# Sums of weight quadrants made in DRAM by transfers that add, in place of additions on VectorE

## The chip, the cores and the metric

The kernel runs on one core of one Trainium2 chip, as one program with one launch. The metric is the time of one execution on the device in microseconds, the median over runs; lower is better.

## The reference

One layer of a hybrid trunk on x of 1024 tokens by 1024 channels, float32 throughout. What bears on this case is the input projection and what reads it:

```python
u = rms_norm(h, norm_w)
proj = u @ w_in
q, f_logit, i_in, g_hg, u_pool, g_pool, xbc, dt_raw, z = jnp.split(
    proj, [int(v) for v in np.cumsum(IN_SPLITS)[:-1]], axis=-1)
o_hg = group_rms_norm(hgrn2_mixer(q, f_logit, i_in, lb), hg_norm_w, HG_HEADS) * jax.nn.silu(g_hg.astype(jnp.float32))
o_pool = pool_mixer(u_pool, pool_w, pool_scale) * jax.nn.silu(g_pool.astype(jnp.float32))
y_ssd = ssd_mixer(xbc, dt_raw, conv_w, conv_b, dt_bias, a_log, d_skip) * jax.nn.silu(z.astype(jnp.float32))
...
h = h + mixed @ w_out
gate = jax.nn.sigmoid(h @ w_pg)
return h + gate * (p_i @ w_pe)
```

w_in has 6668 columns. The change concerns the 1024 columns of u_pool and g_pool (four pairs of 128-column blocks) and 1024 of the columns of z and g_hg (two pairs of 256-column blocks).

## The kernel before, in words

Every float32 operand of a product is split into a high part, rounded to the matmul type (a CAST on ScalarE, L139), and a remainder (a subtraction on VectorE, L140). `mm3` (L163) then makes three matmuls per block: high by high, and each high by the other remainder. uh and ul hold the two parts of the normalised, transposed u, 8 row tiles of 128 tokens.

**The start.** x is loaded in 8 row tiles by SP. For a tile t, `x_norm` (L196) takes the sum of squares on ScalarE (L198), makes the factor rsx on POOL in two small steps, a tensor_scalar and a power (`rstd`, L124, lines L126 and L127), and multiplies on VectorE (L200). `x_turn` (L202) transposes the tile on PE (L208) and splits it into uh and ul (L216, L217). `tm_tile` then makes the tile's first product, the first slab of values. The order of VectorE, ScalarE and POOL in this part is written by hand for its own instructions (`manual_schedule`, L242): the sum of squares of tile t+3 stands behind the splitting of tile t+1. PE's order is transposes of tile t+1, then the product of tile t. Everything after the first slab needs all 8 tiles.

**The Strassen stage.** Six products of u with pairs of column blocks are made with 7 half-size products each in place of 8. u is taken in quadrants; `build_sums` (L281) makes four sums of u's quadrants and splits them. For the weights, with the quadrants b11, b12, b21, b22, four sums are needed: t1 = b12 - b11, t3 = b22 - b12, t2 = t3 + b11, t4 = b21 - t2. `st_cm_w(j0, j1)` (L307) loads two blocks and makes the sums on VectorE (L315, L316, L319, L320) between the splits, for the pairs (26, 27), (30, 31), (28, 29), (32, 33). `st_cm` (L327) makes the seven products and puts them together from PSUM with copies on ScalarE (L340) and additions on VectorE (L344). `st_tm(s0, s1, fin)` (L361) does the same for the two pairs of 256-column blocks, (5, 6) and (7, 2), with its own loads into the arena `big` (L368) and additions at L373.

**Queues.** Raw weights come through `wload` (L130), two buffers of 128x1072, and the split parts go to four buffers each of hi and lo. The arena hands out the slab that has been free longest; whoever writes it waits for its last reader. Stores to pod (L529) and vd (L229) and loads share the queue of SP. Outside of the start a scheduler sets each engine's order; `high_priority` (L138, L314, L318, L343, L372) pulls splits, additions and evacuations forward in it. POOL issues no transfer in this kernel; besides the powers it only fills a few tiles.

Of the kernel before, what the change touches and what calls it, by code (L numbers as in the profile page):

```python
# [77 lines left out]
def body(ctx: ExitStack, tc: tile.TileContext, x, pT, wcm, wtm, wdt, wo, wg, we, nw, fw, cst, prm, out):  # L78
# [228 lines left out]
    def st_cm_w(j0, j1):  # L307

        r0, r1 = wload(wcm[j0], 1024), wload(wcm[j1], 1024)
        b11, b21, b12, b22 = r0[:, :512], r0[:, 512:1024], r1[:, :512], r1[:, 512:1024]  # L310
        T_, Th = bg.take(2048)
        t1, t3, t2, t4 = (T_[:, i * 512 : i * 512 + 512] for i in range(4))
        w0 = wsplit(r0, 1024)
        with tc.high_priority(offset=WPRIO):  # L314
# [2 lines left out]
        w1 = wsplit(T_[:, :1024], 1024)
        with tc.high_priority(offset=WPRIO):  # L318
            V.tensor_tensor(out=t2, in0=t3, in1=b11, op=ALU.add)  # L319
            V.tensor_tensor(out=t4, in0=b21, in1=t2, op=ALU.subtract)  # L320
        w2 = wsplit(T_[:, 1024:], 1024)
        w3 = wsplit(b22, 512)
        bg.give(Th)
# [3 lines left out]
    def st_cm(W, o0, o1):  # L327
# [27 lines left out]
        add_(o1[:, h1], X)  # L355
# [1 line left out]
        add_(o1[:, h0], Y)
# [3 lines left out]
    def st_tm(s0, s1, fin):  # L361

        src = lambda s, i: wtm[s * 2 + i]
        taken = []

        def load(s, i):
            z, h = bg.take(1024)
            nc.sync.dma_start(z, src(s, i))  # L368
            return z, h

        def add(o, x, y, op=ALU.subtract):
            with tc.high_priority(offset=WPRIO):  # L372
                V.tensor_tensor(out=o, in0=x, in1=y, op=op)  # L373
# [735 lines left out]
```

## Time and profile before

| what | value |
|---|---|
| median of 3 runs | 1053.25 us (1051.63 to 1054.33) |
| the profiled execution, its own time | 1054.85 us |
| its span | 1053.0 us |
| mean granted clock of TensorE | 0.994 |
| PE busy | 1027.2 us (98%) |
| VectorE busy | 620.3 us (59%), 1156 instructions |
| ScalarE busy | 447.9 us (43%) |
| POOL busy | 39.9 us (4%), 69 instructions |
| DMA, mean over the span | 79 GB/s |

The profile is of one execution. Its span is the time in which the engines work; 1.85 us of the execution's own time lie around it. A busy time is the sum over an engine's instructions. Matmuls are pipelined, so that a busy PE need not be a PE at its peak: how many matmuls start in a stretch says more. The granted clock is the share of TensorE's full clock (2.4 GHz) that the throttle let through; its other level is half of that.

### The profile page before, as it was taken

The page shows a single profiled execution, that of the slowest core. Times are in us where ns is not written, and L with a number is a line of the kernel's source. Part 1 is how long each engine was busy: PE and PEld are TensorE (multiplying, and loading weights), DVE is VectorE, ACT ScalarE, POOL GpSimd, SP SyncE. Part 2 cuts the span into 40 slices and gives each one's busy share as a digit, 9 for nine tenths or more (in the row PEclk, how much of TensorE's full clock was granted, in tenths as well). Part 3 has the DMA queues.
Part 4 walks back from the last instruction along what each step waited for, and adds up shares of the span by engine and source line. Part 5 has one row for each costly group of instructions (what it writes and reads, how often), then busy time and mean ns, then how long its engine had stood idle before and what let it go on. Part 6 is the DMA issues. An engine that isn't in the chain of part 4 may idle for free.

```text
span 1053.0 us, 19902 instructions
## 1 busy us (share of the span) xinstructions
PE 1027.2 (98%) x8364; PEld 923.7 (88%) x8364; DVE 620.3 (59%) x1156; ACT 447.9 (43%) x904; POOL 39.9 (4%) x69
## 2 busy tenths in 40 slices
PE   8999999999999999999999999999999999999997
PEld 7998787999777787778878787899999999999997
DVE  6874677333368766875686858788422542454434
ACT  6442434445432344235475756697200420243323
POOL 2000000000000000001000000004000000000001
PEclk9999999999999999999999999999999999999998
DMA  7311123216501100110121212343232141111003
GB/s 293 128 66 63 40 100 119 83 61 200 163 22 41 41 22 21 52 41 21 59 72 57 85 40 81 121 139 96 93 118 87 50 141 41 41 41 41 2 21 141
DMA packets 41434, 82.73 MB, mean 79 GB/s; under 512 B 4000, under 2 KB 26880, under 8 KB 41088
## 3 DMA queue, kind: packets, MB, share of 16 engines
q1 hardware_dynamic: 41200, 81.40, 23.1%
q8 instruction: 65, 1.06, 0.4%
q14 instruction: 25, 0.20, 0.1%
q10 hardware_dynamic: 144, 0.07, 0.0%
HBM read 67.76 MB, written 13.68 MB: 77 GB/s over the span
## 4 chain that ended last, share of the span: by engine, by line
PE 81%; DVE 11%; ACT 3%; DMA 3%; issue 1%; POOL 0%; SPq 0%; POOLq 0%; ACTq 0%; DVEq 0%
PE b_pj L166 19%; PE b_pj L165 19%; PE b_pj L167 19%; DVE ar L582 5%; PE b_mx L165 3%; PE b_mx L167 3%; PE b_mx L166 3%; PE b_mx L806 1%; DVE lo L140 1%; PE b_sc L704 1%; PE b_mx L699 1%; PE b_mx L701 1%; DVE blk L601 1%; PE b_sc L167 1%; PE b_sc L166 1%; PE b_sc L165 1%
## 5 line engine op out<-in xcount | busy, mean ns | idle before, releaser
L165 PE MATMUL b_pj<-hi,uh 128*128 128x256 f32 (+1 forms) x1088 | 309.9, 285 | 0.4 <-ACT uh L216 0.4
L166 PE MATMUL b_pj<-lo,uh 128*128 128x256 f32 (+1 forms) x1088 | 307.3, 282 | 0.4 <-DVE lo L140 0.4
L167 PE MATMUL b_pj<-hi,ul 128*128 128x256 f32 (+1 forms) x1088 | 306.6, 282 | 0.2 <-DVE ul L217 0.2
L166 PEld LDWEIGHTS b_pj<-lo,uh 128*128 128x128 f32 x1088 | 205.8, 189 | 1.1 <-DVE lo L140 0.9
L165 PEld LDWEIGHTS b_pj<-hi,uh 128*128 128x128 f32 x1088 | 205.7, 189 | 0.8 <-ACT uh L216 0.6
L167 PEld LDWEIGHTS b_pj<-hi,ul 128*128 128x128 f32 x1088 | 205.5, 189 | 0.4 <-DVE ul L217 0.4
L166 PE MATMUL b_pj<-ul,hi 128*128 128x512 f32 x416 | 168.8, 406 | 0.0
L165 PE MATMUL b_pj<-uh,hi 128*128 128x512 f32 x416 | 168.3, 404 | 0.0
L167 PE MATMUL b_pj<-uh,lo 128*128 128x512 f32 x416 | 167.8, 403 | 0.0
L139 ACT CAST hi<-raw 128x1024 fp32r<-128x1024 f32 (+1 forms) x72 | 73.9, 1026 | 175.6 <-PE b_pj L167 99.0
L140 DVE TENSOR_TENSOR lo<-raw,hi 128x1024 fp32r<-128x1024 f32 (+1 forms) x72 | 85.9, 1194 | 103.5 <-ACT hi L139 91.7
L582 DVE TENSOR_TENSOR ar<-ar 128x512 f32<-128x512 f32 (+8 forms) x168 | 93.9, 594 | 6.5 <-PE b_sc L673 5.0
L166 PEld LDWEIGHTS b_pj<-ul,hi 128*128 128x128 f32 x416 | 78.2, 188 | 17.7
L165 PEld LDWEIGHTS b_pj<-uh,hi 128*128 128x128 f32 x416 | 78.2, 188 | 16.9
L167 PEld LDWEIGHTS b_pj<-uh,lo 128*128 128x128 f32 x416 | 78.2, 188 | 16.7
L748 DVE SCALAR_TENSOR_TENSOR ar<-ar,pr 128x1021 f32<-128x1021 f32 (+2 forms) x42 | 53.7, 1279 | 0.6
L954 DVE TENSOR_TENSOR big<-xr,b_pj 128x256 f32<-128x256 f32 x32 | 13.4, 419 | 50.6 <-PE b_pj L167 50.6
L782 ACT ACTIVATE E<-E,sm 128x128 f32<-128x128 f32 x96 | 32.0, 392 | 25.3 <-DMA E<-cumd 21.0
L956 DVE TENSOR_TENSOR big<-big,b_pj 128x256 f32<-128x256 f32 x32 | 13.4, 419 | 43.5 <-PE b_pj L167 43.5
L1001 ACT ACTIVATE junk<-sg 128x256 f32<-128x256 f32 x32 | 13.4, 418 | 40.2 <-DVE sg L999 40.2
L140 DVE TENSOR_TENSOR lo<-big,hi 128x1024 fp32r<-128x1024 f32 x18 | 21.9, 1222 | 14.0 <-ACT hi L139 14.0
L739 ACT COPY ar<-b_pj 128x512 f32<-128x512 f32 x28 | 16.2, 580 | 31.9 <-PE b_pj L167 31.8
(260 smaller groups left out, 1716.1 us busy)
## 6 DMA issues: line engine op xcount, KB each, us to landing
raw<-wcm SPq DMA_DIRECT2D x34, 512.0 KB, 3.2
raw<-wo SPq DMA_DIRECT2D x16, 512.0 KB, 3.8
raw<-wtm SPq DMA_DIRECT2D x12, 512.0 KB, 3.2
E<-cumd SPq DMA_DIRECT2D x32, 192.0 KB, 3.1
x<-x SPq DMA_DIRECT2D x8, 512.0 KB, 9.4
gzd<-sg SPq DMA_DIRECT2D x32, 128.0 KB, 2.3
xr<-x SPq DMA_DIRECT2D x32, 128.0 KB, 2.3
raw<-wg SPq DMA_DIRECT2D x8, 512.0 KB, 3.4
```

Source lines behind the costliest of these rows:

```text
L139: A.copy(hi[:, :width], raw[:, :width])
L140: V.tensor_tensor(out=lo[:, :width], in0=raw[:, :width], in1=hi[:, :width].bitcast(F32), op=ALU.subtract)
L165: T.matmul(out=o, lhsT=sh, rhs=mh, start=first, stop=False, skip_group_check=more)
L166: T.matmul(out=o, lhsT=sh, rhs=ml, start=False, stop=False, skip_group_check=more)
L167: T.matmul(out=o, lhsT=sl, rhs=mh, start=False, stop=last, skip_group_check=more)
L582: mul = lambda o, x, y: V.tensor_tensor(out=o, in0=x, in1=y, op=ALU.mult)
L739: A.copy(xp[:, c], b)
L748: V.scalar_tensor_tensor(out=y[:, d:], in0=xp[:, : S - d], scalar=cw(i), in1=y[:, d:], op0=ALU.mult, op1=ALU.add)
L782: A.activation(E[:, i, :], E[:, i, :], AF.Relu, scale=-1.0, bias=cum[:, r0 + i : r0 + i + 1])
L954: V.tensor_tensor(out=H[:, t, qc], in0=xr, in1=b, op=ALU.add)
L956: V.tensor_tensor(out=H[:, t, qc], in0=H[:, t, qc], in1=b, op=ALU.add)
L1001: A.activation(junk, sg, AF.Square, accum_out=ssf[:, q, t : t + 1])
```

## The change

Six tiles in DRAM are added, four `tcd` of 128x2048 (four sums of 512 columns) and two `ttd` of 128x4096 (four of 1024). A new function `sums_by_dma`, called once per pair after the start's part in the program, fills them with eight transfers each, all issued by POOL: plain copies and transfers that add their source to what is in the destination. Since a transfer can only add, the sums are those with plus signs throughout (t3 = b22 + b12, t1 = b11 + b12, t2 = t3 + b11, t4 = t2 + b21), and the signs move to the other side: to `build_sums`, and to the copies and additions that put the products together. `st_cm_w` and `st_tm` load the finished sums through `wload` and hold no additions. Their loads into the arena are gone.

```diff
+    PAIRS_C = ((26, 27), (30, 31), (28, 29), (32, 33))
+    PAIRS_T = ((5, 6), (7, 2))
+    tcd = [dp.tile([P, 2048], F32, name=f"tcd{i}") for i in range(4)]
+    ttd = [dp.tile([P, 4096], F32, name=f"ttd{i}") for i in range(2)]
+
+    def sums_by_dma(d, n, b11, b12, b21, b22):
+        t1, t3, t2, t4 = (d[:, i * n : i * n + n] for i in range(4))
+        add = lambda o, i: nc.gpsimd.dma_start(out=o, in_=i, accum_op=ALU.add)
+        nc.gpsimd.dma_start(out=t3, in_=b22)
+        nc.gpsimd.dma_start(out=t1, in_=b11)
+        add(t3, b12)
+        add(t1, b12)
+        nc.gpsimd.dma_start(out=t2, in_=t3)
+        add(t2, b11)
+        nc.gpsimd.dma_start(out=t4, in_=t2)
+        add(t4, b21)
...
     xst.close()
+    for d, (j0, j1) in zip(tcd, PAIRS_C):
+        sums_by_dma(d, 512, wcm[j0][:, :512], wcm[j1][:, :512], wcm[j0][:, 512:], wcm[j1][:, 512:])
+    for d, (s0, s1) in zip(ttd, PAIRS_T):
+        sums_by_dma(d, 1024, wtm[2 * s0], wtm[2 * s1], wtm[2 * s0 + 1], wtm[2 * s1 + 1])
...
-        V.tensor_tensor(out=Q22, in0=Q21, in1=Q22, op=ALU.add)
+        V.tensor_tensor(out=Q22, in0=Q22, in1=Q21, op=ALU.subtract)
         V.tensor_tensor(out=Q21, in0=Q11, in1=Q21, op=ALU.subtract)
-        V.tensor_tensor(out=Q11, in0=Q22, in1=Q11, op=ALU.subtract)
-        V.tensor_tensor(out=Q12, in0=Q12, in1=Q11, op=ALU.subtract)
+        V.scalar_tensor_tensor(out=Q11, in0=Q22, scalar=-1.0, in1=Q11, op0=ALU.mult, op1=ALU.subtract)
+        V.scalar_tensor_tensor(out=Q12, in0=Q11, scalar=-1.0, in1=Q12, op0=ALU.mult, op1=ALU.subtract)
...
-        r0, r1 = wload(wcm[j0], 1024), wload(wcm[j1], 1024)
...
-            V.tensor_tensor(out=t1, in0=b12, in1=b11, op=ALU.subtract)
-            V.tensor_tensor(out=t3, in0=b22, in1=b12, op=ALU.subtract)
...
+        w0 = wsplit(wload(wcm[j0], 1024), 1024)
+        w1 = wsplit(wload(tcd[i][:, :1024], 1024), 1024)
+        w2 = wsplit(wload(tcd[i][:, 1024:], 1024), 1024)
+        w3 = wsplit(wload(wcm[j1][:, 512:], 512), 512)
...
-        cp_(o1[:, h1], Y)
+        cp_(o1[:, h1], Y, -1.0)
...
-        add_(o1[:, h1], X)
+        add_(o1[:, h1], X, ALU.subtract)
...
+        srcs = {1: wtm[2 * s0], 2: wtm[2 * s0 + 1], 3: wtm[2 * s1 + 1]}
+        for n, z in enumerate((5, 7, 6, 4)):
+            srcs[z] = ttd[i][:, n * 1024 : n * 1024 + 1024]
...
+        def want_(z):
+            W[z] = wsplit(wload(srcs[z], 1024), 1024)
+
+        for z in (1, 6, 7):
+            want_(z)
...
-                    V.tensor_tensor(out=o[t], in0=o[t], in1=Y[t][:, :256], op=ALU.add)
+                    V.tensor_tensor(out=o[t], in0=o[t], in1=Y[t][:, :256], op=ALU.subtract)
```

The scheduler puts the new transfers into POOL's order among the steps of the start. Lines of the changed kernel are 18 higher there: L144 and L145 are the two small steps of `rstd`, L123, L124, L127 and L129 the plain transfers of `sums_by_dma`, L122 the adding ones. DMASW0 to DMASW7 are the eight semaphores on which POOL's transfers land. POOL's order at the start before, from the last fill on; the two small steps of a tile follow each other with nothing between:

```order
L119 MEMSET blk1_97 128x256
L126 ISA
L126 TENSOR_SCALAR rsx_109<-ssx_108 128x1 [waits Activation_49]
L127 TENSOR_TENSOR rsx_109<-rsx_109,negh_94 128x1 [waits Pool_49]
L126 TENSOR_SCALAR rsx_109<-ssx_108 128x1 [waits Activation_49]
L127 TENSOR_TENSOR rsx_109<-rsx_109,negh_94 128x1 [waits Pool_49]
```

and with the change, to the power of the first tile:

```order
L137 MEMSET blk1_103 128x256
L123 DMA tcd0_94<-wcm 128x512
L124 DMA tcd0_94<-wcm 128x512
L123 DMA tcd1_95<-wcm 128x512
L124 DMA tcd1_95<-wcm 128x512
L122 DMA tcd0_94<-wcm 128x512 [waits DMASW0_49]
L122 DMA tcd0_94<-wcm 128x512 [waits DMASW1_49]
L122 DMA tcd1_95<-wcm 128x512 [waits DMASW2_49]
L144 ISA
L144 TENSOR_SCALAR rsx_115<-ssx_114 128x1 [waits Activation_49]
L127 DMA tcd0_94<-tcd0_94 128x512 [waits DMASW4_49]
L145 TENSOR_TENSOR rsx_115<-rsx_115,negh_100 128x1 [waits Pool_49]
```

Eight transfers now stand ahead of the first tile's power, four of them behind a landing, and one of these stands between its two small steps. At the last tiles of the start, before, POOL goes from the last power to the fills of `big`:

```order
L126 TENSOR_SCALAR rsx_109<-ssx_108 128x1 [waits Activation_49]
L127 TENSOR_TENSOR rsx_109<-rsx_109,negh_94 128x1 [waits Pool_49]
L126 TENSOR_SCALAR rsx_109<-ssx_108 128x1 [waits Activation_49]
L127 TENSOR_TENSOR rsx_109<-rsx_109,negh_94 128x1 [waits Pool_49]
L554 MEMSET big_77 128x1024 [waits DMAHW3_49,DVE_49]
```

and with the change, from the power of the sixth tile to that of the eighth:

```order
L145 TENSOR_TENSOR rsx_115<-rsx_115,negh_100 128x1 [waits Pool_49]
L122 DMA tcd2_96<-wcm 128x512 [waits DMASW2_49]
L122 DMA tcd3_97<-wcm 128x512 [waits DMASW4_49]
L144 TENSOR_SCALAR rsx_115<-ssx_114 128x1 [waits Activation_49]
L122 DMA ttd0_98<-wtm 128x1024 [waits DMASW1_49]
L145 TENSOR_TENSOR rsx_115<-rsx_115,negh_100 128x1 [waits Pool_49]
L122 DMA ttd0_98<-wtm 128x1024 [waits DMASW5_49]
L129 DMA tcd3_97<-tcd3_97 128x512 [waits DMASW7_49]
L144 TENSOR_SCALAR rsx_115<-ssx_114 128x1 [waits Activation_49]
L127 DMA ttd0_98<-ttd0_98 128x1024 [waits DMASW3_49,DMASW0_49]
L145 TENSOR_TENSOR rsx_115<-rsx_115,negh_100 128x1 [waits Pool_49]
```

Each of the last two powers has three transfers ahead of it, all of which wait for a landing; 12 more follow the eighth power. On VectorE, the small chain (tile sm) that leads to the matmul of L479 had the additions of the second pair between its steps:

```order
L467 SCALAR_TENSOR_TENSOR sm_1021<-sm_1021 128x96 x4
L315 TENSOR_TENSOR big_77<-raw_1181,raw_1179 128x512
L316 TENSOR_TENSOR big_77<-raw_1181 128x512
L467 SCALAR_TENSOR_TENSOR sm_1021<-sm_1021 128x96
L319 TENSOR_TENSOR big_77<-big_77,raw_1179 128x512
L467 SCALAR_TENSOR_TENSOR sm_1021<-sm_1021 128x96
L320 TENSOR_TENSOR big_77<-raw_1179,big_77 128x512
L468 SCALAR_TENSOR_TENSOR sm_1021<-sm_1021 128x96
```

and has nothing between them now:

```order
L452 SCALAR_TENSOR_TENSOR sm_1075<-sm_1075 128x96 x6
L453 SCALAR_TENSOR_TENSOR sm_1075<-sm_1075 128x96
L455 SCALAR_TENSOR_TENSOR sm_1075<-sm_1075 128x96
L460 TENSOR_TENSOR sm_1075<-sm_1075,nega_1093 128x96
```

The four additions are gone from there, and the steps of sm follow each other directly.

## Rows read from the trace of the kernel before

**Rows 1.** The page: busy time by engine, and the chain that ended last.
```profile
PE 1027.2 (98%) x8364; PEld 923.7 (88%) x8364; DVE 620.3 (59%) x1156; ACT 447.9 (43%) x904; POOL 39.9 (4%) x69
...
PE 81%; DVE 11%; ACT 3%; DMA 3%; issue 1%; POOL 0%; SPq 0%; POOLq 0%; ACTq 0%; DVEq 0%
```

**Rows 2.** Busy time in stretches: length, engines' busy us (instructions), granted clock, DMA share, GB/s.
```profile
84.00:98.00 14.00, 13.33 (x76) 11.34 (x76) 9.57 (x26) 4.38 (x9) 0.00 (x0) 1.00 0.16 56
175.00:190.00 15.00, 13.02 (x94) 12.32 (x93) 5.81 (x6) 5.49 (x11) 0.00 (x0) 0.89 0.42 141
190.00:215.00 25.00, 25.00 (x213) 25.00 (x212) 13.03 (x17) 11.72 (x24) 1.92 (x2) 1.00 0.29 101
```

**Rows 3.** Timeline of PE: start us, us, instruction, idle time before it and what ended it.
```profile
96.91 0.46 PE L479 MATMUL b_mx<-sm,cs 128*128 128x96 f32 x2 [0.67 <-DVE sm L475]
...
181.88 0.50 PE L165 MATMUL b_pj<-hi,sh 128*128 128x256 f32 x2 [1.13 <-ACT hi L139]
...
183.14 0.39 PE L166 MATMUL b_pj<-lo,sh 128*128 128x256 f32 x1 [0.52 <-DVE lo L140]
```

**Rows 4.** Timeline of POOL at the start: the powers of tiles 1, 2, 3 and 8.
```profile
6.06 0.56 POOL L127 TENSOR_TENSOR rsx<-rsx,negh 128x1 f32<-128x1 f32 x1
...
11.32 0.55 POOL L127 TENSOR_TENSOR rsx<-rsx,negh 128x1 f32<-128x1 f32 x1
...
13.33 1.41 POOL L127 TENSOR_TENSOR rsx<-rsx,negh 128x1 f32<-128x1 f32 x1
...
30.51 0.55 POOL L127 TENSOR_TENSOR rsx<-rsx,negh 128x1 f32<-128x1 f32 x1
```

**Rows 5.** Timeline at the start: tile 1's multiply and transposes, and tile 8's transposes.
```profile
6.65 1.28 DVE L200 SCALAR_TENSOR_TENSOR x<-x,rsx,nwb 128x1024 f32<-128x1024 f32 x1 [6.65 <-POOL rsx L127]
...
7.99 1.09 PE L208 MATMUL b_mx<-ident,x 128*128 128x128 f32 x8 [0.77 <-DVE x L200]
...
34.83 1.04 PE L208 MATMUL b_mx<-ident,x 128*128 128x128 f32 x8
```

**Rows 6.** Groups of VectorE: shape and count, then busy us and mean ns of one.
```profile
L373 DVE TENSOR_TENSOR big<-raw,big 128x1024 f32<-128x1024 f32 x4 | 4.9, 1222 | 5.8 <-DMA raw<-wtm 3.0 <-DMA big<-wtm 2.8
L315 DVE TENSOR_TENSOR big<-raw 128x512 f32<-128x512 f32 x4 | 2.7, 686 | 2.6 <-DMA raw<-wcm 2.6
L507 DVE TENSOR_TENSOR big<-big 128x1023 f32<-128x1023 f32 x4 | 4.9, 1222 | 0.1
L513 DVE SCALAR_TENSOR_TENSOR big<-big 128x1021 f32<-128x1021 f32 x1 | 1.2, 1216 | 0.0
```

**Rows 7.** DMA issues: queue, count, KB of each, median us from issue to landing.
```profile
raw<-wtm SPq DMA_DIRECT2D x12, 512.0 KB, 3.2
x<-x SPq DMA_DIRECT2D x8, 512.0 KB, 9.4
xr<-x SPq DMA_DIRECT2D x32, 128.0 KB, 2.3
vd<-vs SPq DMA_DIRECT2D x24, 128.0 KB, 1.7
big<-vd SPq DMA_DIRECT2D x6, 512.0 KB, 6.3
```

**Rows 8.** SP's first issue (start, us), and POOL's instructions: min/median/max in ns, or busy and mean.
```profile
0.72 0.39 SPq L107 DMA_DIRECT2D x<-x  x1
L127 POOL TENSOR_TENSOR rsy<-rsy,negh x8: 1006/1007/1829, 710.6 to 734.4; 128x4 f32<-128x4 f32 x8
L127 POOL TENSOR_TENSOR rsh<-rsh,negh x6: 1635/1640/2675, 315.4 to 493.8; 128x8 f32<-128x8 f32 x6
L554 POOL MEMSET big<- 128x1024 f32 x2 | 1.9, 958 | 177.1 <-DVE lo L140 176.0 <-ACT sg L540 1.2
```

**Rows 9.** Busy time in stretches of the start, columns as in rows 2.
```profile
0.00:42.00 42.00, 37.73 (x276) 35.03 (x277) 29.26 (x38) 25.85 (x48) 7.60 (x23) 1.00 0.58 214
...
4.00:8.00 4.00, 3.23 (x10) 2.23 (x9) 1.28 (x1) 1.26 (x3) 0.75 (x2) 1.00 1.02 357
```

More of the change, by code (lines that the diff above doesn't have):

```diff
@@ L305, in body, with st_cm_w @@
     bg.give(ufh)
-    def st_cm_w(j0, j1):
-        r0, r1 = wload(wcm[j0], 1024), wload(wcm[j1], 1024)
[L310 to L314, printed above, removed]
-            V.tensor_tensor(out=t1, in0=b12, in1=b11, op=ALU.subtract)
-            V.tensor_tensor(out=t3, in0=b22, in1=b12, op=ALU.subtract)
[L317 to L323, printed above, removed]
+    def st_cm_w(i):
+        j0, j1 = PAIRS_C[i]
+        w0 = wsplit(wload(wcm[j0], 1024), 1024)
+        w1 = wsplit(wload(tcd[i][:, :1024], 1024), 1024)
+        w2 = wsplit(wload(tcd[i][:, 1024:], 1024), 1024)
+        w3 = wsplit(wload(wcm[j1][:, 512:], 512), 512)
         part = lambda w, i: tuple(z[:, i * 512 : i * 512 + 512] for z in w)
@@ L336, in prod, with cp_, add_ @@
                 mm3(b, wh[:, w], wl[:, w], ah[:, k, :], al[:, k, :], first and k == 0, k == 3, not first)
-        def cp_(o, b):
+        def cp_(o, b, scale=1.0):
             with tc.high_priority(offset=EPRIO):
-                A.copy(o, b)
-        def add_(o, b):
+                A.activation(o, b, AF.Copy, scale=scale)
+        def add_(o, b, op=ALU.add):
             with tc.high_priority(offset=EPRIO):
-                V.tensor_tensor(out=o, in0=o, in1=b, op=ALU.add)
+                V.tensor_tensor(out=o, in0=o, in1=b, op=op)
         prod(X, 1, True)
@@ L354, in st_cm, with st_tm @@
         prod(X, 7, False)
[L355 removed]
+        add_(o1[:, h1], X, ALU.subtract)
         prod(Y, 3, False)
[L357 removed]
+        add_(o1[:, h0], Y, ALU.subtract)
         prod(X, 4, False)
         cp_(o0[:, h1], X)
[L361 to L373, printed above, removed]
[L375 to L401 removed]
+    def st_tm(i, fin):
+        s0, s1 = PAIRS_T[i]
+        srcs = {1: wtm[2 * s0], 2: wtm[2 * s0 + 1], 3: wtm[2 * s1 + 1]}
+        for n, z in enumerate((5, 7, 6, 4)):
+            srcs[z] = ttd[i][:, n * 1024 : n * 1024 + 1024]
+        W = {}
+        def want_(z):
+            W[z] = wsplit(wload(srcs[z], 1024), 1024)
+        for z in (1, 6, 7):
+            want_(z)
         cs_ = [bg.take(1024) for _ in range(3)]
@@ L415, in st_tm @@
         X = [bank("mx") for _ in range(4)]
-        w4()
+        want_(4)
         for o, i in ((c11, 1), (c12, 6), (c22, 7)):
@@ L419, in st_tm @@
                 with tc.high_priority(offset=EPRIO):
-                    A.copy(o[t], X[t][:, :256])
-            {1: w5, 6: w3, 7: w2}[i]()
+                    A.activation(o[t], X[t][:, :256], AF.Copy, scale=1.0 if i == 1 else -1.0)
+            want_({1: 5, 6: 3, 7: 2}[i])
         for t in prod(X, 4, False):
@@ L498, in body @@
         st_cm(W, U0, U1)
-        W = st_cm_w(30 + g0, 31 + g0)
+        W = st_cm_w(1 + g0)
         pos = []
@@ L524, in body @@
         if g0 == 0:
-            W = st_cm_w(28, 29)
+            W = st_cm_w(2)
         for (g, U, Uh), Gt in zip(pos, (G0, G1)):
@@ L535, in body @@
     gzd = dp.tile([P, NT, 1024], F32, name="gzd")
-    for i, slabs in enumerate(((5, 6), (7, 2))):
+    for i in range(2):
         def gz_fin(t, n, b, i=i):
```

29 lines of the change are left out of this document (3 added, 26 removed).

## The prediction, made blind

> **What bounds the kernel now.** I read the page first, for the engine that is full. TensorE (PE) is busy for 98% of the span and holds 81% of the chain that ended last; VectorE (DVE) is busy for 59% and holds 11% of that chain [rows 1]. So an addition taken off VectorE is worth only the time in which PE stands still for it. The second view is the table of stretches: where do matmuls come slower than they can? In the stretch 190 to 215 us PE starts 213 matmuls in 25.0 us, 8.52 per us. In 175 to 190 us it starts 94, which at that rate need 11.0 us: 4.0 us are lost there, the largest loss around the additions. In 84 to 98 us PE is idle for 0.67 us [rows 2]. The third view is the timeline of PE in these two places. At 181.88 us it waited 1.13 us for a cast of weights, at 183.14 us 0.52 us for a remainder, and in the stretch the granted clock was 0.89: after these gaps TensorE ran at the lower of its levels (1.2 GHz) for a while, which is 15 x 0.11 = 1.65 of the 4.0 us. At 96.91 us it waited 0.67 us for a small VectorE chain, between whose steps four additions stand [rows 3].
>
> The fourth view is the start, since the new transfers are issued from the POOL queue, and there POOL works for the critical path. For each of the 8 row tiles of x, POOL makes the factor rsx in two small steps (L126, L127). The first power starts at 6.06 us, the second at 11.32, the eighth at 30.51 [rows 4]. VectorE's x_norm multiply (L200) waits for it, then come the transposes on PE: first power 6.06, first transposes 7.99, so 1.93 us behind. The transposes of the eighth tile start at 34.83 us, because PE is then busy with the tiles before; so the eighth power may come as late as 34.83 - 1.93 = 32.9 us before it moves anything [rows 5].
>
> **The change part by part.** *Removed from VectorE:* 16 additions of 128x512 (four lines of four, 686 ns mean) and 8 of 128x1024 (1.22 us) [rows 6]: 11.0 + 9.8 = 20.8 us of work, nearly all under matmuls. In the order of VectorE the four additions between the small steps that lead to the matmul at 96.91 us are gone, so its 0.7 us goes. In 160 to 180 us a raw quadrant had to land, be added twice and only then be cast; now each sum lands ready in a raw buffer. The first two are loaded while the product before still runs, and the copies of product 1 no longer land in an arena slab that still waits for its store to pod. So I take out the whole 4.0 us. Gain: 0.7 + 4.0 = **4.7 us**, and no more, since PE has no other gap near the additions. What is late next there: the sums pass through two raw buffers, 3.2 us a load [rows 7], against 5.6 us (48 matmuls at 8.52 per us) for each product that reads one, so nothing.
>
> *Moved signs:* copies with a scale of -1, subtractions for additions, and scalar_tensor_tensor for tensor_tensor in build_sums cost what the old forms cost; a scalar_tensor_tensor of 1021 elements takes 1.22 us as the addition of 1023 elements does [rows 6]. Nothing.
>
> *Added:* 48 transfers from POOL, each sum a chain of dependent steps. In POOL's order 36 of them stand ahead of the eighth power, and most wait for an earlier transfer to land. POOL takes its queue in order, so a waiting transfer holds the x_norm step behind it, and VectorE, PE and ScalarE behind that. The trace has no transfer issued by POOL, none that adds, and none from DRAM to DRAM, so three prices are bounded.
> - Issue on POOL: at least SP's 0.39 us. At most 1.64 us, POOL's longest usual small instruction (the power of 8 columns). I take **1.0 us**, the power of 4 columns (1.007) or a memset of 1024 columns (0.958), because POOL's own work is the nearest [rows 8].
> - Landing of a plain 256 KB transfer, counted from the end of its issue: between 1.7 - 0.4 = 1.3 us (128 KB to DRAM) and 3.1; I take 2.2, below the 3.2 - 0.4 = 2.8 us of 512 KB [rows 7].
> - Landing of an adding one: it reads two sources, as many bytes as a 512 KB load. Between 1.3 and 6.3 - 0.4 = 5.9 us (six loads queued at once); I take 3.1 [rows 7]. For the 512 KB pieces of ttd I take 1.3 times as much.
> - Until 16 us all landings are doubled: the DMA engines are then at a share of 1.02 and an x tile takes 9.4 us instead of 3.2 [rows 7, 9].
>
> Now POOL's queue, step by step. It is free at 1.3 us. Four plain issues end at 2.3, 3.3, 4.3 and 5.3. The first lands at 2.3 + 4.4 = 6.7; the adding transfer that waits for it is issued by 7.7 and lands at 13.9; two more adding ones are issued by 9.7. The copy into t2 waits until 13.9 and is issued by 14.9: only then comes the first power, at **14.9** instead of 6.06. The copy lands at 19.3, and three issues end by 18.5 meanwhile; the next adding one is issued by 20.3 and lands at 23.4; three more issues end by 23.3; the copy into t4 goes out from 23.6 to 24.6, and the second power starts at **24.6** instead of 11.32. From there to the eighth power POOL issues 20 transfers (20 us) and runs six pairs of small steps (0.83 us each, 5.0); where a landing is later than the queue, it costs 1.2 more. The eighth power starts at 24.6 + 26.2 = **50.8**.
>
> The last two tiles of the slab and all that follows stand behind it as before, so the delay is 50.8 - 32.9 = **17.9 us**. PE, which waits between the tiles, will see its clock fall; I add one stretch like that of 175 to 190 us, 1.7 us. The sum: 17.9 + 1.7 - 4.7 = **+14.9 us**. The profiled execution took 1054.85 us (span 1053.0 and 1.85 around it), which gives 1069.8. It stood 1.6 us above the median of the runs, 1053.25, so the forecast is **1068**.
>
> With SP's issue price and the same landings, the eighth power is at 39.8 us, and the delay 6.9 instead of 17.9. The Trainium skill (DMA: Bandwidth & Descriptors, section on latency and other measured facts) gives about 1 us to the first byte for transfers issued from GpSimd, whose descriptors software writes, and 0.6 us for the others. By the page, taken as an issue price, the sum is the +14.9; by SP's row it is about +4.
>
> Do the sums come late for their readers? POOL's last transfer, the last of the second slab's sums, lands near 78 us by these prices, and that slab's sums are read only past the place of 181 us [rows 3]; those of tcd0, read first, are done by 33 us, before the eight tiles are. So no load waits.
>
> **The rivals.**
> 1. *Adding transfers are slow* (5.9 us, plain 3.1). Then the chains, not the issues, fill POOL's queue: eighth power at 65.9, delay 33, sum +30: **1083**. For it: x loads take 9.4 us when the engines are shared, and an adding transfer also has to read what it writes [rows 7]. Against: later the DMA share is low, 0.16 in 84 to 98 us [rows 2].
> 2. *POOL is held back by VectorE.* The power of the third tile took 1.41 us instead of 0.55 while a VectorE subtraction ran [rows 4]. VectorE is busy for 29.26 of the first 42 us [rows 9]; if every issue waited for the half of a 1.25 us instruction in 7 of 10 cases, that is 0.44 us more an issue: eighth power at 62.7, delay 29.8, sum +26.8: **1080**. The Trainium skill (SBUF — State Buffer, section Who interferes with whom) has VectorE and GpSimd lock a shared pair of ports, and descriptor writing starved by some VectorE forms, but a tensor_tensor only against GpSimd's reads; by that the issue would not wait here, and I give it little.
> 3. *POOL issues as fast as SP* (0.39 to 0.42 us) with the landings above: delay 6.9, of which the clock takes nothing, sum +2.2: **1055.5**, within what can be told from no change.
> 4. *Faster:* the transfers are cheap throughout, 0.42 us to issue and 1.3 to land. Then the eighth power is at 28.8 us, no later than now, no start-up delay is left, and the 4.7 us stay: **1048.5**. It decides at an eighth power of 34.4 us: up to there at least 3.2 us of gain survive. For it: most landings of 128 KB are under 2.3 us; against it: the DMA engines are full exactly while the first chains run [rows 9].
>
> That the additions stay on VectorE is not a case: in its order the lines L315 to L320 and L373 are gone.
>
> **How the numbers follow.** My forecast has a chance of 0.50, rival 1 0.17, rival 2 0.05, rival 3 0.16, rival 4 0.12. About 0.3% (3.2 us) is what a measurement of this kernel can tell from no change. Slower by more: 0.50 + 0.17 + 0.05 = 0.72; within it: 0.16; faster: 0.12. The range reaches from the gain of rival 4 nearly whole (1049) to rival 1 with POOL's issues a little dearer, 1.2 us (eighth power at 70.3, 4 us more: 1087, taken as 1088). With both upper bounds, 1.64 and 5.9 us, the eighth power would be at 80 and the time 1098; that is left out, as is a gain beyond 4.7 us.
>
> **What would show it.** In the profile after: the eight powers on POOL near 15, 25, 27, 33, 37, 42, 46 and 51 us; VectorE's x multiply waiting for POOL for some 20 us more in total; PE much less than full in the first 55 us, with a lower granted clock; the transposes of the eighth tile near 52.7 us; no gap at the place of 181 us (then near 200); VectorE with 24 additions and about 21 us less. I am wrong if the eighth power starts before 34 us, if PE waits in the Strassen stage for a load of tcd or ttd, or if the gap ahead of the slab products stays.

## The result and the profile after

The changed kernel takes **1105.86 us** (median of 3 runs, 1105.21 to 1108.68) against 1053.25 before: ratio 1.0508, 95% interval 1.0473 to 1.0544. The forecast was 1068 us with a range of 1049 to 1088. The direction was right, the size was not: 52.6 us are lost where 14.9 were forecast. The profiled execution took 1105.21 us, with a span of 1103.4 us and a mean granted clock of 0.975.

The page of the kernel after, busy time by engine and the transfers' groups (queue, count, KB of each, median us from issue to landing), and the DMA queues (packets, MB, share of the 16 engines' span):

```profile
PE 1035.5 (94%) x8364; PEld 931.7 (84%) x8364; DVE 601.9 (55%) x1132; ACT 448.9 (41%) x904; POOL 73.2 (7%) x117
...
q1 hardware_dynamic: 43216, 87.69, 24.3%
q0 software_dynamic: 5888, 16.78, 7.9%
...
tcd<-wcm POOLq DMA_DIRECT2D x24, 256.0 KB, 9.5
ttd<-wtm POOLq DMA_DIRECT2D x12, 512.0 KB, 9.0
...
x<-x SPq DMA_DIRECT2D x8, 512.0 KB, 17.5
...
tcd<-tcd POOLq DMA_DIRECT2D x8, 256.0 KB, 6.1
```

VectorE has lost its 24 additions (1156 to 1132 instructions) and 18.4 us of busy time [rows 1], so the change does what it says. The moved signs cost nothing: each of the three altered operations of `build_sums` takes 2.28 to 2.29 us, before 2.28. (That a transfer can only add is a premise of the change; no run tries another form.) But a transfer of weights into tcd lands 9.5 us after the start of its issue, and the loads of x take 17.5 us in place of 9.4 [rows 7].

The timeline of POOL in the kernel after: the first transfers, the first two powers, and the eighth.

```profile
1.33 0.76 POOL L123 DMA_DIRECT2D tcd<-wcm  x1
...
9.97 0.89 POOL L122 DMA_DIRECT2D tcd<-wcm  x1 [6.30 <-DMA tcd<-wcm]
12.48 1.71 POOL L122 DMA_DIRECT2D tcd<-wcm  x2 [1.62 <-DMA tcd<-wcm]
14.34 0.19 POOL L144 TENSOR_SCALAR rsx<-ssx 128x1 f32<-128x1 f32 x1
20.01 0.59 POOL L127 DMA_DIRECT2D tcd<-tcd  x1 [5.48 <-DMA tcd<-wcm]
20.62 0.60 POOL L145 TENSOR_TENSOR rsx<-rsx,negh 128x1 f32<-128x1 f32 x1
...
37.59 0.59 POOL L145 TENSOR_TENSOR rsx<-rsx,negh 128x1 f32<-128x1 f32 x1
...
82.92 0.58 POOL L145 TENSOR_TENSOR rsx<-rsx,negh 128x1 f32<-128x1 f32 x1
```

The first power waits in the queue exactly where the forecast put it, between two halves of its own step: its tensor_scalar ran at 14.34, then POOL stood 5.48 us for a landing ahead of the copy into t2, and only then came the power, at 20.62 us (6.06 before) [rows 4]. The eighth came at 82.92 us (30.51 before), after a forecast of 50.8.

Who waited for it, in the waits of VectorE and PE over the first 160 us (us in total, times, longest), and the stretches of the start (columns as in [rows 2]):

```profile
DVE x L218 <- POOL rsx L145: 63.0, 8, 21.3
...
PE b_mx L226 <- DVE x L218: 44.6, 8, 15.0
...
PE b_pj L183 <- ACT vs L246: 3.5, 1, 3.5
...
PE b_mx L464 <- DVE sm L460: 0.3, 1, 0.3
```

```profile
0.00:42.00 42.00, 13.89 (x47) 11.49 (x48) 6.22 (x6) 8.70 (x13) 14.69 (x29) 0.67 0.95 260
42.00:84.00 42.00, 25.09 (x169) 23.91 (x168) 13.82 (x24) 13.34 (x29) 18.20 (x31) 0.83 0.98 176
84.00:120.00 36.00, 31.52 (x235) 31.34 (x236) 30.73 (x20) 13.71 (x19) 6.60 (x10) 0.88 0.95 246
120.00:152.00 32.00, 32.00 (x236) 30.43 (x235) 13.45 (x30) 9.09 (x16) 1.36 (x2) 1.00 0.47 132
```

VectorE's x multiply waits 63.0 us for POOL's powers, PE 44.6 us for the x multiply. PE starts 47 instructions in the first 42 us where it started 276 [rows 9], and its granted clock is 0.67 and 0.83 there, so part of what it does is done at 1.2 GHz. The DMA engines are full not until 16 us but until 120, and although they are full they move only 176 to 260 GB/s.

In milestones of PE: the last transposes of the start come 50.9 us later than before, and the last pooling matmul (L518 before, L503 after) 57.1 us later, since a stretch at 1.2 GHz and the wait of 3.5 us at 102.89 us came on top. From there to the first matmul behind the two slabs (L595, now L580) 3.9 us are won back, where PE no longer stands still ahead of the slab products; that is the gain the change was forecast to bring. Another 1.4 us come back between 727 and 735 us of before, where of these two profiles only that of before has a stretch of lower clock (0.96 in 720 to 760 us); the rest comes in small steps, and the end is 50.4 us late.

### The profile page after: what moved, and what is told of

Read it like the earlier page. It is cut to its first block, busy times and chain, and to the rows that moved or that the text cites. A ratio compares the mean times of both kernels' runs of the same rounds, so it can differ in the third digit from the quotient of the medians.

```text
span 1103.4 us, 19969 instructions
## 1 busy us (share of the span) xinstructions
PE 1035.5 (94%) x8364; PEld 931.7 (84%) x8364; DVE 601.9 (55%) x1132; ACT 448.9 (41%) x904; POOL 73.2 (7%) x117
## 3 DMA queue, kind: packets, MB, share of 16 engines
q0 software_dynamic: 5888, 16.78, 7.9%
## 4 chain that ended last, share of the span: by engine, by line
PE 76%; DVE 9%; ACT 3%; DMA 2%; issue 0%; POOL 0%; SPq 0%; POOLq 0%; ACTq 0%; DVEq 0%
PE b_pj L183 18%; PE b_pj L184 18%; PE b_pj L185 18%; DVE ar L567 5%; PE b_mx L183 3%; PE b_mx L185 3%; PE b_mx L184 3%; PE b_mx L791 1%; DMA E<-cumd 1%; PE b_sc L689 1%; PE b_mx L684 1%; PE b_sc L183 1%; PE b_sc L185 1%; PE b_sc L184 1%; PE b_mx L686 1%; DVE blk L586 1%
## 5 line engine op out<-in xcount | busy, mean ns | idle before, releaser
L183 PE MATMUL b_pj<-hi,uh 128*128 128x256 f32 (+1 forms) x1088 | 313.2, 288 | 3.5 <-ACT vs L246 3.5
L185 PE MATMUL b_pj<-hi,ul 128*128 128x256 f32 (+1 forms) x1088 | 309.8, 285 | 0.0
L183 PEld LDWEIGHTS b_pj<-hi,uh 128*128 128x128 f32 x1088 | 209.1, 192 | 4.1 <-ACT vs L246 3.7
L184 PEld LDWEIGHTS b_pj<-lo,uh 128*128 128x128 f32 x1088 | 208.8, 192 | 0.2
L158 DVE TENSOR_TENSOR lo<-raw,hi 128x1024 fp32r<-128x1024 f32 (+1 forms) x90 | 108.0, 1200 | 125.1 <-ACT hi L157 122.8
L157 ACT CAST hi<-raw 128x1024 fp32r<-128x1024 f32 (+1 forms) x90 | 92.5, 1029 | 198.4 <-PE b_pj L185 99.5
L226 PE MATMUL b_mx<-ident,x 128*128 128x128 f32 x64 | 12.1, 351 | 44.6 <-DVE x L218 44.6
L226 PEld LDWEIGHTS b_mx<-ident,x 128*128 128x128 f32 x64 | 9.7, 182 | 46.6 <-DVE x L218 27.6
L234 ACT CAST uh<-b_mx 128x512 fp32r<-128x512 f32 x32 | 17.5, 590 | 74.5 <-PE b_mx L226 56.2
L218 DVE SCALAR_TENSOR_TENSOR x<-x,rsx,nwb 128x1024 f32<-128x1024 f32 x8 | 10.3, 1285 | 63.0 <-POOL rsx L145 63.0
L939 DVE TENSOR_TENSOR big<-xr,b_pj 128x256 f32<-128x256 f32 x32 | 13.5, 421 | 49.9 <-PE b_pj L185 49.9
## 6 DMA issues: line engine op xcount, KB each, us to landing
x<-x SPq DMA_DIRECT2D x8, 512.0 KB, 17.5
```

The costliest lines, as they stand in the source:

```text
L157: A.copy(hi[:, :width], raw[:, :width])
L158: V.tensor_tensor(out=lo[:, :width], in0=raw[:, :width], in1=hi[:, :width].bitcast(F32), op=ALU.subtract)
L183: T.matmul(out=o, lhsT=sh, rhs=mh, start=first, stop=False, skip_group_check=more)
L184: T.matmul(out=o, lhsT=sh, rhs=ml, start=False, stop=False, skip_group_check=more)
L185: T.matmul(out=o, lhsT=sl, rhs=mh, start=False, stop=last, skip_group_check=more)
L226: T.transpose(out=b[:, i * P : (i + 1) * P], in_=xt[:, k * P : (k + 1) * P], identity=ident)
```

## The experiments

Theory A: POOL's queue, taken in order, holds the steps of x_norm behind chains of transfers. Theory B: the transfers fill the DMA engines, and every load and store beside them is late. They need not exclude each other; the runs were to tell the shares apart, then what in the chains is dear (issue, dependence, bytes, adding), and then whether a place without the loss exists. Times of before beside each run were 1052.7 to 1053.8 us. Four slips in the expectations: e3_plain speaks of 32 adding transfers, there are 24 (four of each pair's eight); e5_ttd_late speaks of 30 transfers ahead of the powers and e8_small of 44, in the traces there are 32 and 48; and the wait "near 54 us" begins at 47.2 and ends at 50.44 us, the lower clock behind it lasts to 56.

**1. All transfers behind the eighth power.**

```diff
-    for d, (j0, j1) in zip(tcd, PAIRS_C):
+    with tc.issue_after(rs_last[0].ins):
+        for d, (j0, j1) in zip(tcd, PAIRS_C):
...
```

> All 48 transfers are queued on POOL behind the eighth power of x_norm, everything else as in the change. Theory A (POOL's queue: x_norm's small steps stand behind transfers that wait): the start is that of before again, eighth power near 30.5 us, transposes of the eighth tile near 35, and the time is that of before less the two gaps the change closes, 1048 to 1053 us. Theory B (the transfers fill the DMA engines, and loads and stores land late wherever they run): the sums now run from 31 to about 120 us beside the weight loads and the stores to vd, PE waits there instead, 1060 us or more. Theory C (the sums come late for their readers once they start at 31 us): PE waits for a raw buffer of tcd0 near 85 to 97 us, some 10 us, about 1060.

Measured: 1060.23 us (1056.16 to 1064.59, 4 runs), ratio 1.0077 (1.0051 to 1.0104). The eighth power is at 30.48 us and the first 40 us are those of before: 45.6 of the 52.6 us are gone. The run moves two things at once, the place in POOL's queue and the crowd beside the loads of x (9.3 us again); experiment 2 separates them. What is left begins at 43 us. ScalarE, PE and the stretch in this run:

```profile
49.03 1.08 ACT L157 CAST hi<-raw 128x1072 fp32r<-128x1072 f32 x1 [5.85 <-DMA raw<-wdt]
```

```profile
50.44 0.58 PE L183 MATMUL b_pj<-hi,uh 128*128 128x256 f32 x1 [3.24 <-ACT vs L248]
```

```profile
40.00:60.00 20.00, 16.76 (x120) 16.55 (x120) 16.09 (x9) 6.14 (x9) 6.58 (x10) 0.83 1.00 249
```

The weight load issued at 40.70 us lands only at 49, and its cast holds ScalarE's queue. The copy that frees PE's accumulator stands behind the cast. This is theory B at a smaller price, and near what B and C had expected of the time (C's wait for a raw buffer of tcd0 does not show on PE). The profiled execution is the fastest of the four (1056.16); what the other three lost beyond it is not seen.

**2. The factor of x_norm on VectorE, the transfers where they were.** The power becomes three Newton steps on VectorE, in the changed kernel and, as a control, in the one before.

```diff
-        rstd(rsx[:, t : t + 1], ssx[:, t : t + 1], D)
+        V.tensor_scalar(out=v, in0=ssx[:, t : t + 1], scalar1=1.0 / D, scalar2=EPS, op0=ALU.mult, op1=ALU.add)
+        V.tensor_scalar(out=y, in0=v, scalar1=-0.5, scalar2=1.5, op0=ALU.mult, op1=ALU.add)
+        for _ in range(3):
+            V.scalar_tensor_tensor(out=z, in0=y, scalar=y, in1=v, op0=ALU.mult, op1=ALU.mult)
+            V.tensor_scalar(out=z, in0=z, scalar1=-0.5, scalar2=1.5, op0=ALU.mult, op1=ALU.add)
+            V.tensor_tensor(out=y, in0=y, in1=z, op=ALU.mult)
```

> The transfers stay where the change put them, but the factor of x_norm is made on VectorE (three Newton steps in place of the power), so POOL holds nothing that x needs. Theory A (the queue alone): the delay of 50 us goes nearly whole, 1052 to 1060 us. Theory B (the full DMA engines alone): x tiles still land in 17 us instead of 9, the eighth tile is late by tens of us, 1090 us or more. Between them the delay splits: what is left over the time of before is the share of the DMA engines.

> Control: the kernel before with the same factor of x_norm on VectorE. Some 90 small VectorE instructions in the first 35 us, of well under 0.2 us each and where VectorE is idle for a third of the time: within 3 us of 1053 under every theory. If it is slower than that, the figure is taken off the one with the transfers.

Measured: 1081.68 us with the transfers, 1064.17 without (one run each). The control misses its expectation by 8 us: eleven more VectorE steps between a tile's sum of squares and its multiply cost time on the path. Against the control the transfers cost 17.5 us, so with POOL out of x's way and the DMA engines as full (a share of 0.96 in the first 42 us), about a third of the 52.6 us stays and some 35 go: theory A holds for the larger part, as far as single runs can tell. The waits of PE and of ScalarE in the run with the transfers, and between them PE's wait for x in the control:

```profile
PE b_pj L183 <- ACT vs L253: 15.5, 2, 11.7
PE b_mx L233 <- DVE x L225: 7.7, 5, 2.5
```

```profile
PE b_mx L215 <- DVE x L207: 10.0, 8, 2.8
```

```profile
ACT nega L464 <- DMA pr<-prm: 14.4, 1, 14.4
...
ACT hi L157 <- DMA raw<-wdt: 9.6, 2, 7.6
```

Not x is late now (7.7 us of waits, 10.0 in the control) but a load that ScalarE, in its own order, stands in front of: the parameter table pr, then the weights of dt.

**3. What in the chains is dear.** Four runs with the transfers issued by POOL from the start, as in the change. e3_plain makes the adding ones plain and so leaves the additions out; e4_free has 48 plain ones that depend on nothing; e8_small keeps chains and adding but moves 64 columns each; e11_small_free has 48 independent plain ones of 64 columns.

```diff
-        add = lambda o, i: nc.gpsimd.dma_start(out=o, in_=i, accum_op=ALU.add)
+        add = lambda o, i: nc.gpsimd.dma_start(out=o, in_=i)
```

> The 32 adding transfers are plain ones in the same places and the same chains, so the summed quadrants are wrong (copies of the last source). Theory D (adding is what makes a transfer dear): a 256 KB transfer lands in 3 to 5 us instead of 9.5, the eighth power is near 50 us instead of 83 and the time near 1072. Theory E (any transfer from DRAM to DRAM is slow beside full engines): landings of 8 to 10 us, eighth power above 70 us, 1095 us or more.

```diff
+        f = free[(tcd + ttd).index(d)]
+        for i, z in enumerate((b22, b11, b12, b12)):
+            nc.gpsimd.dma_start(out=f[:, i * n : i * n + n], in_=z)
+        for i, z in enumerate((b22, b11, b21, b21)):
+            nc.gpsimd.dma_start(out=d[:, i * n : i * n + n], in_=z)
```

> In the place of the chains 48 plain transfers of the same sizes that read only weights, so none depends on another; the sums are left out (their quadrants hold copies). What still makes POOL wait is that its ninth transfer waits for its first, with eight in flight. Theory A, strict (the chains' dependences fill the queue): the eighth power comes near 30 to 40 us and the time is 1053 to 1065. Theory H (eight in flight beside full DMA engines is a queue as slow as the chains: 48 transfers of 350 KB at some 200 GB/s): eighth power at 55 us or later, 1075 to 1090.

```diff
-        t1, t3, t2, t4 = (d[:, i * n : i * n + n] for i in range(4))
+        t1, t3, t2, t4 = (d[:, i * n : i * n + 64] for i in range(4))
+        b11, b12, b21, b22 = (z[:, :64] for z in (b11, b12, b21, b22))
```

> The transfers keep their number, their chains and their adding, but move 64 columns each instead of 512 or 1024, and the readers load weights of the same size instead, so the sums are left out. The DMA engines are then nearly as free as before. Theory B (full DMA engines): eighth power near 31 to 36, 1053 to 1056 us. Theory A (issue and dependence in POOL's order): 44 transfers at 0.55 to 0.85 us stand ahead of the eighth power, 31 us, and some fifteen waits of 1 to 2 us: eighth power at 45 to 60, delay 12 to 27 us, 1063 to 1078 us.

```diff
+        for i, z in enumerate((b22, b11, b12, b12, b22, b11, b21, b21)):
+            nc.gpsimd.dma_start(out=d[:, i * 64 : i * 64 + 64], in_=z[:, :64])
```

> 48 plain transfers of 64 columns that depend on nothing (sums left out, readers load weights of the same size). Theory A by its parts (small chains cost 22 us, large independent ones 23, large plain chains 33): with neither bytes nor dependences only the issues are left, 0.55 us each and eight in flight: eighth power at 32 to 42 us, 1053 to 1062 us. If it is 1070 or more, the number of transfers on POOL alone makes most of the 22 us.

| the transfers are | of 48 ahead of the eighth power | eighth power | time | over before |
|---|---|---|---|---|
| 64 columns, independent, plain (e11_small_free) | 48 | 42.3 us | 1060.92 | 7.8 |
| 64 columns, chains, adding (e8_small) | 48 | 59.7 us | 1076.33 | 22.5 |
| full size, independent, plain (e4_free) | 37 | 52.0 us | 1076.81 | 23.0 |
| full size, chains, plain (e3_plain) | 36 | 65.8 us | 1086.31 | 33.0 |
| full size, chains, adding (the change) | 36 | 82.9 us | 1105.86 | 52.6 |

All but the last are single runs, and runs with late transfers scattered by 5 to 11 us (experiments 1 and 5), so the steps are read roughly, with the eighth power beside the time. The scheduler also put all 48 small transfers ahead of the eighth power and only 36 or 37 of the full size, so the two sizes are not to be taken from one another. At small size the 48 issues alone cost some 8 us (net of what the slabs win back, as all times here), as theory A by its parts said, and dependence and adding together 15, as theory A said of e8_small. At full size dependence costs 10, and adding 20 more. e4_free has the time of theory H, with a power 3 us earlier: with no chain and nothing added, eight transfers in flight beside full engines put the power back by 21.5 us, against 52.4 in the change. e3_plain falls between its two theories (landings of 6.6 and 6.2 us, 1086 us), so adding is dear, but not all of the price.

The page of e3_plain, its transfers and their queue:

```profile
q0 software_dynamic: 4864, 16.78, 5.1%
...
tcd<-wcm POOLq DMA_DIRECT2D x24, 256.0 KB, 6.6
ttd<-wtm POOLq DMA_DIRECT2D x12, 512.0 KB, 6.2
```

The same 16.78 MB took 5.1% of 1084.5 us on all 16 engines, 55 us, and 7.9% of 1103.4 in the change, 87 us. Half of the bytes are moved by adding transfers; if the plain half costs 27.7 us in both, the adding half costs 59.5, **2.1 times** a plain one (an estimate). The engines are free earlier for it: where the change has a share of 0.95 in 84 to 120 us, e3_plain has

```profile
84.00:120.00 36.00, 36.00 (x291) 36.00 (x290) 23.21 (x17) 13.63 (x18) 2.06 (x4) 0.96 0.51 167
```

**4. Only the slabs' transfers behind the eighth power.** The loop over tcd stays.

```diff
-    for d, (s0, s1) in zip(ttd, PAIRS_T):
+    with tc.issue_after(rs_last[0].ins):
+        for d, (s0, s1) in zip(ttd, PAIRS_T):
...
```

> Only the 16 transfers of the two slabs (ttd) go behind the eighth power; the 32 of tcd stay. Theory A: the powers still stand behind 30 of the transfers, so most of the delay stays: eighth power at 65 to 80 us, 1085 to 1100 us. Theory B (bytes: the 8.4 MB of ttd are half of all that is moved): the delay halves, 1075 to 1080 us.

Measured: 1106.61 us (one run), eighth power at 80.74. The power still stands behind the chains of tcd, and the landings of those are as slow as ever (9.2 us). The time is 6 us beyond the end of theory A's range. Against theory B the run says less than was meant: in the change only 5 of the 16 transfers of ttd stood ahead of the eighth power (and 31 of tcd), so the bytes ahead of it fell from 10.7 to 8.4 MB and not by half, and a count of bytes is hardly tested by it.

**5. Behind the eighth power, one chain after the other; and the first alone, then the rest.**

```diff
+    behind = rs_last[0]
     for d, (j0, j1) in zip(tcd, PAIRS_C):
+        with tc.issue_after(behind.ins):
+            behind = sums_by_dma(d, 512, wcm[j0][:, :512], wcm[j1][:, :512], wcm[j0][:, 512:], wcm[j1][:, 512:])
```

> As the run with all transfers behind the eighth power, but one chain after the other, so that at most three transfers are in flight. Theory F (what that run still lost is the crowd: with eight transfers in flight a weight load took 8 us instead of 3 and PE waited 3.2 us at about 54 us for it): that wait goes or falls under 1 us, a 256 KB transfer that adds lands in 4 to 6 us, and the time is 1048 to 1054 us, level with before or up to 0.4% faster. Rival G (any transfer beside it delays the load as much): the wait near 54 us stays, 1056 us or more. Rival C (sums late for their readers): the six chains end near 31 + 6 x 25 = 180 us and PE waits for a raw buffer ahead of the slab products.

```diff
     for d, (j0, j1) in zip(tcd, PAIRS_C):
+        with tc.issue_after(behind.ins):
+            last = sums_by_dma(d, 512, wcm[j0][:, :512], wcm[j1][:, :512], wcm[j0][:, 512:], wcm[j1][:, 512:])
+        if d is tcd[0]:
+            behind = last
```

> All transfers behind the eighth power; the chain of tcd0 runs alone, the other five behind it and among each other as the scheduler lays them. Theory (the two late versions lost at opposite ends: with all chains at once a weight load at 41 us took 8 us and PE waited 3.2 us near 54; with one chain at a time the sums of tcd3 and ttd0 came 20 and 13 us late for their readers): tcd0 is done near 60 us with no PE wait before it, the other chains end near 150 us, before the first slab's sum is read near 165 to 180, and PE waits for neither. 1049 to 1054 us. Rival G (any crowd of transfers delays some load that PE needs, wherever it runs): a wait of 2 to 4 us turns up between 60 and 150 us, 1054 to 1060 us.

Measured: 1071.37 us (ratio 1.0157, 1.0131 to 1.0182) and 1063.85 us (1.0108, 1.0079 to 1.0137), neither better than e1_late (1060.23), whose crowd they were to thin; the first is slower, the second not clear of it (their ranges of times overlap). The wait at 50 us is gone in both (PE 20.00 and 19.98 busy in 40 to 60 us), as theory F wanted, but rival C comes in its place. The waits of SP's queue in e6_chain:

```profile
SPq L150 <- DMA tcd<-wcm: 35.1, 4, 20.2
...
SPq L150 <- DMA ttd<-wtm: 25.6, 4, 13.5
```

The sums come 20.2 and 13.5 us late for their loads, and PE stands still for 9.1 us until 168 us, and for 5.5 us until 203. In e9_first_alone a load waits 11.9 us for its sum and PE 7.4 us until 122.64. So a chain that runs nearly alone is no quick one. POOL in e6_chain, from the second half of the third chain:

```profile
106.71 0.56 POOL L127 DMA_DIRECT2D tcd<-tcd  x1 [5.76 <-DMA tcd<-wcm]
110.78 0.81 POOL L122 DMA_DIRECT2D tcd<-wcm  x1 [3.52 <-DMA tcd<-tcd]
117.42 0.54 POOL L129 DMA_DIRECT2D tcd<-tcd  x1 [5.83 <-DMA tcd<-wcm]
121.55 0.81 POOL L122 DMA_DIRECT2D tcd<-wcm  x1 [3.58 <-DMA tcd<-tcd]
```

With one transfer of POOL in flight a plain 256 KB copy takes 4.1 us from the start of its issue to the next step (106.71 to 110.78, 117.42 to 121.55), an adding one 6.6 (110.78 to 117.42); beside the first of the three the adding transfer before it was still landing until 108.02. Over the whole run steps that stand alone in this way take 4.0 to 4.6 us on tcd for a plain transfer (four of them) and 5.7 to 8.7 for an adding one (four). Six steps of a chain stand in a row, and a chain of tcd takes 29 to 32 us.

**6. Only the two slabs' sums by transfers, from 31 us and from 98 us.** The sums of tcd go back to VectorE, as additions. In the second kernel the chains wait for a small POOL copy of a column of cum.

```diff
+    late = cp.tile([P, 1], F32, name="late")
+    behind = G.tensor_scalar(out=late, in0=cum[:, :1], scalar1=1.0, scalar2=0.0, op0=ALU.mult, op1=ALU.add)
+    for d, (s0, s1) in zip(ttd, PAIRS_T):
+        with tc.issue_after(behind.ins):
+            behind = sums_by_dma(d, 1024, wtm[2 * s0], wtm[2 * s1], wtm[2 * s0 + 1], wtm[2 * s1 + 1])
```

> Only the two slabs' sums are made by transfers, behind the eighth power and one chain after the other; the sums of tcd stay on VectorE (with the changed signs). Theory (what the change can gain is the gap of PE ahead of the slab products near 181 us; the additions of tcd were hidden): 16 transfers end near 31 + 2 x 36 = 103 us, long before they are read, at most three in flight, no PE wait near 54 us and none near 181: 1049 to 1052.5 us. Rival (the gap's 2.3 us come back as another wait, or the loads beside the chains pay them): 1053 to 1056 us.

> As the run with the slabs' sums alone, but POOL issues them only once the decay sums (cum) are there, near 100 us, where the DMA engines are at a share of 0.2 and nothing of the start is left (a small POOL copy of one column of cum stands ahead of them). Theory (the 2.3 us of the gap at 181 were earned in that run and paid back by the waits near 54 and 97 us, 1.6 and 1.8 us, which the transfers beside the loads of v caused): both waits are as before, the chains run from 100 to about 170 us, and the time is 1050 to 1052 us, 0.1 to 0.3% faster than before. Rival (there was nothing to earn: PE's gap comes back at another place): ratio 0.999 to 1.001, and PE waits for a sum or shows a gap elsewhere.

Measured: 1054.48 us from 31 us on (ratio 1.0004, 0.9992 to 1.0015: no difference), and **1046.64 us from 98 us on (1045.71 to 1048.35; ratio 0.9946, 0.9933 to 0.9958): faster than both kernels**, and 3 us more than was expected of it. In the first, the waits of PE from 30 us on are

```profile
PE b_mx L476 <- DVE sm L472: 1.8, 1, 1.8
PE b_pj L182 <- ACT vs L247: 1.6, 1, 1.6
```

where before has 0.7 us for the one and none for the other, and the clock is at its lower level from 100.6 to 104.0 us: by the first matmul behind the slabs, gain and loss have nearly cancelled, as its rival said. In the second both are as before, and in its stretches

```profile
98.00:120.00 22.00, 22.00 (x90) 16.23 (x89) 14.98 (x25) 8.11 (x16) 4.57 (x7) 1.00 0.81 193
...
175.00:190.00 15.00, 15.00 (x128) 15.00 (x127) 5.91 (x5) 7.80 (x15) 1.91 (x2) 1.00 0.53 184
190.00:215.00 25.00, 25.00 (x215) 25.00 (x214) 9.61 (x16) 11.20 (x22) 0.00 (x0) 1.00 0.55 175
```

PE starts 128 matmuls in 175 to 190 us where before started 94, at a clock of 1.00 and not 0.89 [rows 2]. Up to the pooling matmuls of 164 us the two profiles agree within 0.4 us; the first matmul behind the slabs (282.1 us) is 5.05 us earlier, 4.7 of it won there. That much of the 6.1 us between the medians is traced. Behind 526 us the profile wins another 3.4 us, nearly all in steps under 0.03 us and with the same granted clock as before; the 700 matmuls from 802 us on take 81.9 us here and 82.4 to 82.5 in every other trace, so this is not laid to the transfers, and its cause is open. The 2.3 us in the expectations were counted from the small chain's matmul (L479, now L464), ahead of which the change starts 683 matmuls and before 690; counted from the pooling matmuls they are the 3.9 us above. The DMA engines are busy at 0.81 in 98 to 120 us, and PE is busy through the whole stretch.

## Why the prediction was wrong

**The mechanism and its place: right.** The profile shows what the prediction listed: POOL's queue holds each power behind landings, VectorE's multiply waits for POOL, PE runs short and at 1.2 GHz, the gap ahead of the slab products is gone, and no load of tcd or ttd kept PE waiting (POOL's last transfer went out at 125 us). Experiments 1 and 2 show that POOL's queue makes the larger part of the loss. In the sum, the delay of 17.9 us was 50.9, the clock's 1.7 was 6.2 with what came on top, and the gain of 4.0 was 3.9.

**The failing step: the landing prices, and with them the delay of 17.9 us.** "Landing of a plain 256 KB transfer ... I take 2.2" and "of an adding one ... I take 3.1", doubled "until 16 us". Measured from the start of the issue, in medians: 6.1 us for the copies within tcd, 9.4 for the eight plain copies of weights into tcd, 9.5 for the 16 adding ones. From its end, as the prediction counts, these are 5.5, 8.5 and 8.6, and the engines are full until 120 us. Three walks through the prediction's own POOL queue, with 0.57 us of issue for a plain and 0.84 for an adding transfer, give estimates of the eighth power. With the prediction's landings it comes at 44 us. With those found when one of POOL's transfers is in flight (3.5 plain and 5.8 adding, e6_chain's 4.1 and 6.6 less the issue, never doubled) it comes at 51, and with those of the change itself at 79, where 82.92 was measured. So most of the error is that the landings were priced for engines that the transfers leave free. The reasons are in the runs. The transfers are their own crowd: all 48 are worth 87 us of all 16 engines, the adding ones 2.1 times as much as plain ones (e3_plain), and in such a crowd a plain transfer lands as late as an adding one (9.4 us in e4_free, where none adds). And even nearly alone an adding one needs about the prediction's upper bound of 5.9, and a plain one more than its 3.1. The bounds came from loads and stores between DRAM and SBUF, the nearest rows there were; a transfer that reads, adds and writes in DRAM is not between them.

The Trainium skill (DMA: Bandwidth & Descriptors, section Anatomy of one DMA — SWDGE (gpsimd) path) fits the time of a GpSimd-issued transfer by 2.0 us plus its bytes over 436,000 per us: for 256 KB an estimate of 2.6 us, near what was taken for a plain one. The 4.1 us measured here with one of POOL's transfers in flight is half as much again, and for adding ones the page gives no figure.

**The doubling: wrong in length.** It rested on x's loads alone; that the new transfers would keep the engines full themselves was not counted. The full engines also made loads and stores beside the start late: 1.7 us were forecast for the clock, 6.2 came between the last transposes and the pooling matmuls (57.1 - 50.9), a wait of 3.5 us among them.

**The issue price: too high.** 1.0 us was taken; POOL's issues last mostly 0.54 to 0.59 us for a plain and 0.80 to 0.93 for an adding transfer. In the forecast the 36 issues made up most of POOL's queue; in e11_small_free 48 of them cost some 8 us.

**The gain: right for its larger part.** 4.0 us were forecast for the gap ahead of the slabs: 3.9 in the change, 4.7 where nothing else disturbs it (e14_slabs_100). Of the 0.7 us at the small VectorE chain 0.4 came.

**The rivals.** Rival 1 (slow adding transfers, chains that fill POOL's queue) comes nearest to what happened; it had 0.17. Its prices of 5.9 and 3.1 us were still too low, and the plain ones were slow as well. The case with all upper bounds, 1098 us, was left out of the range and is nearer than anything in it, but by luck: its landings are too short and its issue of 1.64 us is twice or three times what was measured. Rival 2 (VectorE holds POOL) does not show in the change: the issues of the 16 adding transfers into tcd last 0.814 to 0.928 us, whatever VectorE does meanwhile. In e8_small the adding issues beside a VectorE instruction last 0.99 us in the median and the others 0.85, a third of the 0.44 us that the rival asked for. Rivals 3 and 4 wanted landings that no run has at full size.

## What to carry to other kernels

A transfer in the queue of an engine that also computes for the critical path is paid twice: by its issue, and by every wait that stands in the queue ahead of that engine's own work. Put such transfers behind the last step that others wait for, and count what they do to the DMA engines: here the same 16 transfers won 6 us issued from 98 us on (4.7 of them traced), and nothing issued from 31. Of the hidden additions of tcd only 0.4 us of a PE wait came back, so they were hardly worth moving; the two slabs' sums stood in PE's way, and moving them alone, past the start, made the kernel faster than before.
